# Operands moved within a 512-byte line: input tiles 256 bytes and activations 128 bytes off the weights, yt and yo level with them

## The chip, the cores and the metric

The kernel runs on one core of one Trainium2 chip. The metric is device time in microseconds (us). TensorE (PE in the profile) does the matmuls, VectorE (DVE), ScalarE (ACT) and GpSimd (POOL) the elementwise work, SyncE (SP) issues most DMAs. On-chip memory, SBUF, has 128 partitions, and a tile has the same byte address in each of them. This document speaks of the place of a tile as its address modulo 512, "its byte in a 512-byte line", and of the offset of a matmul as the place of its moving operand less the place of its weights, modulo 512.

## The reference

Two layers of a decoder trunk on x of 512 tokens by 1024 channels, all in float32:

```python
for l in range(DEPTH):                                   # DEPTH = 2
    x = x + 0.5 * swiglu(rms_norm(x, ffn1_norm[l]), ffn1_w_up[l], ffn1_w_down[l])
    h = rms_norm(x, mix_norm[l])
    q, k, v, z, xbc, dt_raw, gate_sb, gate_ssm = jnp.split(h @ w_in[l], IN_SPLITS, axis=-1)
    y_sb  = stick_breaking_attention(q, k, v) @ w_branch_sb[l]       # 4 heads of 128
    y_ssm = mamba2_mixer(z, xbc, dt_raw, ...) @ w_branch_ssm[l]      # 24 heads of 64, 8 groups
    x = x + (sigmoid(gate_sb) * y_sb + sigmoid(gate_ssm) * y_ssm) @ w_out[l]
    x = x + 0.5 * swiglu(rms_norm(x, ffn2_norm[l]), ffn2_w_up[l], ffn2_w_down[l])
return rms_norm(x, final_norm)
# swiglu: gate, up = split(h @ w_up); (silu(gate) * up) @ w_down, 2816 hidden channels
```

## The kernel before, in words

All activations lie with channels on the partitions and the 512 tokens in the free dimension, in blocks of 128 channels. A float32 matrix product is made of three matmuls in a reduced float32 format (`mm3`, lines 315 to 317): each operand is split into a high part and a low part, and high x high, low x high and high x low are accumulated. `mm(ps, a, b)` takes a as the weights, which are loaded into TensorE, and b as the moving operand, which streams through. While one matmul streams, the weights of the next are loaded.

The weights of the model come as a list of units (`unit_order`), a unit being up to 8 blocks of 128x128. Each is fetched to a tile wraw and split by ScalarE into whi (line 282) and by VectorE into wlo (line 284), a few units ahead of their use. `dense` runs a unit: for each block k, `mm3` with the unit's block k as weights and the moving pair of block k. The order of the work is written out by hand; generators that are stepped once a block (`tick`) put the elementwise work between the matmuls.

What moves against the weights, stage by stage:

- the first products of a feed-forward part, the q, k, conv and gate projections: the pair hhi, hlo of the normed input, 512 columns; the attention starts from them
- the rest of the up-projection (`pair_of_blocks`), which works on halves of 256 tokens with combined blocks: hhi and hlo, and the pair th, tl of combined inputs (`combine`), 256 columns
- the down-projection of a feed-forward part: the pair act, act, 512 columns (256 in the last three units, `ending`)
- the branch products: yt (the gated output of the state-space part, twelve pairs) and ohi, olo (of attention, pool yo), 512 columns; yt also holds q, k and v before
- the output projection: mhi, mlo, 512 columns
- v and z (`by_tokens`): here the input pair hhi, hlo is the weights and whi, wlo the moving operand, 512, 408 or 384 columns. For each block of 128 tokens, k = 0 and k = 1 follow each other, and the second lies `pitch` elements further in the unit; in the z block of 408 columns that is 448 elements, 1792 bytes.

Pools are stacked in SBUF from both sides, so the size of each tile sets the place of all that are stacked on it. In the built program they come to lie so (byte in a 512-byte line):

| tiles | before | after |
|---|---|---|
| whi, wlo, wraw | 96 | 96 |
| hhi, hlo, and acc, rs, sq, nones, ntri, upto | 96 | 352 |
| act, and s1, s2, s3, a, c, g of the feed-forward part | 96 | 224 |
| yt, ohi, olo | 480 | 96 |
| th, tl, uv, x | 480 | 480 |
| mhi, mlo, and bT, cT, btok, dec, xs, y of the mixer | 96 | 96 |

Of the kernel before, what the change touches and what calls it, by code (L numbers as in the profile page):

```python
# [8 lines left out]
F32 = mybir.dt.float32  # L9
# [8 lines left out]
P = 128  # L18
SEQ = 512
NT = SEQ // P  # L20
DM = 1024
# [142 lines left out]
class Builder:  # L164
# [298 lines left out]
    def consts(self):  # L463
        nc = self.nc
        c = self.cst
        self.ident = c.tile([P, P], F32, name="ident")
        make_identity(nc, self.ident)
        self.ones = c.tile([P, P], F32, name="ones")
        nc.vector.memset(self.ones, 1.0)
        self.eps = c.tile([P, 1], F32, name="eps")  # L470
        nc.vector.memset(self.eps, EPS)
        self.nones = c.tile([P, P], F32R, name="nones")
        self.ntri = c.tile([P, P], F32R, name="ntri")
        with self.tc.tile_pool(name="cst_tmp", bufs=1, reuse_waits="tile") as tp:
            neg = tp.tile([P, P], F32, name="neg")
            nc.vector.memset(neg, -1.0)
            nc.vector.tensor_copy(self.nones, neg)
            tri = tp.tile([P, P], F32, name="tri")
            nc.gpsimd.affine_select(out=tri, in_=neg, pattern=[[-1, P]], compare_op=ALU.is_ge, fill=0.0,
                                    base=0, channel_multiplier=1)  # L480
            nc.vector.tensor_copy(self.ntri, tri)
        self.upto = c.tile([P, P], F32, name="upto")
        nc.gpsimd.affine_select(out=self.upto, in_=self.ones, pattern=[[1, P]], compare_op=ALU.is_ge, fill=0.0,
                                base=0, channel_multiplier=-1)


    def rsqrt_small(self, v, y):
# [187 lines left out]
    def ending(self, base, act, n, fp):  # L675


        nc, half = self.nc, SEQ // 2
        blocks, units, squares, self.closing = OUT_ORDER[-3:], {}, {}, False
        gain = self.pars[0][:, G_FIN:G_FIN + KB]  # L680

        def block(m, ps, cols):
            x = self.x[m][:, cols]
            nc.vector.scalar_tensor_tensor(x, ps, 0.5, x, op0=ALU.mult, op1=ALU.add)
            yield 1
            sq = self.t(fp, [P, SEQ], "g", bufs=4)[:, :half]
            nc.scalar.activation(sq, x, AF.Square)
            self.closing = m == KB - 1 and cols.start
            if m == KB - 1:
                squares[cols.start] = sq  # L690
                return
            yield 1
            acc = self.acc[:, cols]
            nc.vector.tensor_tensor(acc, acc, sq, op=ALU.add)

        def finish(cols):
            ps = self.t(self.ptr, [P, SEQ], "pt")[:, :half]
            nc.tensor.matmul(ps, self.ones, self.acc[:, cols], start=True, stop=False)
            nc.tensor.matmul(ps, self.ones, squares[cols.start], start=False, stop=True)
            y = self.t(fp, [P, SEQ], "c", bufs=2)[:, :half]  # L700
            t, v = (self.t(fp, [P, SEQ], "a")[:, :half] for _ in range(2))
            nc.scalar.activation(y, ps, AF.Ln, scale=1.0 / DM, bias=self.eps)
            nc.scalar.activation(y, y, AF.Exp, scale=-0.5)
            nc.vector.tensor_scalar(v, ps, 1.0 / DM, EPS, op0=ALU.mult, op1=ALU.add)
            yield 2
            nc.vector.tensor_tensor(t, y, v, op=ALU.mult)
            nc.vector.scalar_tensor_tensor(t, t, -0.5, y, op0=ALU.mult, op1=ALU.mult)
            nc.vector.scalar_tensor_tensor(y, t, 1.5, y, op0=ALU.add, op1=ALU.mult)
            for m in range(KB):
                if m == 2 and not cols.start:  # L710
                    while not self.closing:
                        yield 1
                if m % 2 == 0:
                    yield 1
                r = self.xg[m][:, cols]
                if m in blocks:
                    nc.vector.scalar_tensor_tensor(r, self.x[m][:, cols], gain[:, m:m + 1], y,
                                                   op0=ALU.mult, op1=ALU.mult)
                else:
                    nc.vector.tensor_tensor(r, r, y, op=ALU.mult)  # L720
                (nc.scalar if m % 2 and cols.start else nc.sync).dma_start(self.out[m][:, cols], r)

        for m in blocks:
            self.xg[m] = self.t(self.hp, [P, SEQ], "hhi", F32R).bitcast(F32)
        for h in range(2):
            cols = slice(h * half, (h + 1) * half)
            for i, m in enumerate(blocks):
                pool, tag = (self.pa, "pa") if h and i else (self.pmm, "mm")
                ps = self.t(pool, [P, SEQ], tag)[:, :half]
                if h == 0:  # L730
                    units[m] = self.unit(*base, m)
                hi, lo = units[m]
                for k in range(n):
                    ks = slice(k * P, (k + 1) * P)
                    self.mm3(ps, (hi[:, ks], lo[:, ks]), [a[:, cols] for a in act[k]], k == 0, k == n - 1)
                    if k % 2:
                        self.tick()
                self.spawn(block(m, ps, cols))
            if h == 0:
                self.spawn(finish(cols), 2)  # L740
        while half not in squares:
            self.tick()
        self.spawn(finish(slice(half, SEQ)))
        self.flush()

    def ffn(self, layer, f, gain, gain_next):
        tc = self.tc
        with tc.tile_pool(name=f"act{layer}{f}", bufs=8, reuse_waits="tile") as ap, \
                tc.tile_pool(name=f"sx{layer}{f}", bufs=2, reuse_waits="tile") as self.sx, \
                tc.tile_pool(name=f"ffn{layer}{f}", bufs=3, reuse_waits="tile") as fp:  # L750
            self.gated = {}
            for s, (j0, j1) in enumerate(SLICES):
                act = []
                last = s == len(SLICES) - 1
# [43 lines left out]
    def dt_stage(self, layer):  # L798
# [5 lines left out]
        x = self.dtx.rearrange("p h c -> p (h c)")  # L804
        raw = yield from self.take("raw")
        u, w, adt, cum_t = raw[:, :n], raw[:, n:2 * n], raw[:, 2 * n:3 * n], raw[:n, SEQ - P:]
        self.tok = self.t(self.nrm, [P, 4, HEADS, NT], "sq")
        dt, cum, grown, left = (self.tok[:, i].rearrange("p h c -> p (h c)") for i in range(4))
        na = self.t(mp, [P, HEADS], "na", bufs=1)
        self.tables(True)  # L810
        nc.scalar.activation(u, x, AF.Abs)
# [14 lines left out]
        yield 3  # L826
        pt = self.t(self.ptr, [P, SEQ], "pt")
        nc.tensor.matmul(pt[:, :n], self.upto, adt, start=True, stop=True)
        nc.tensor.matmul(pt[:, n:2 * n], self.ones, adt, start=True, stop=True)
        yield 2  # L830
        nc.vector.tensor_copy(cum, pt[:, :n])
        nc.vector.tensor_tensor(left, pt[:, n:2 * n], cum, op=ALU.subtract)
        self.ecb = self.t(mp, [P, HEADS, NT], "ecb", bufs=1)
        nc.scalar.activation(grown, pt[:, :n], AF.Exp)
        nc.scalar.activation(self.ecb.rearrange("p h c -> p (h c)"), pt[:, n:2 * n], AF.Exp)
        yield 2
        nc.scalar.activation(left, left, AF.Exp)
        pt = self.t(self.ptr, [P, SEQ], "pt")
# [266 lines left out]
    def ssd_group(self, layer, g):  # L1105
# [15 lines left out]
        def heads(ap):  # L1121
            return ap.rearrange("p (h d) -> p h d", d=HD)
# [27 lines left out]
        def inner(c):  # L1150
            pc = self.t(self.ptr, [P, SEQ], "pt")
            pu = pc[:, P:P + GW]
            nc.tensor.matmul(pc[:, :P], bt[:, span(c)], ct[:, span(c)], start=True, stop=True)  # L1153
            if c < NT - 1:
                nc.tensor.matmul(pu, btok[:, c, :], xws[c].rearrange("p h d -> p (h d)"), start=True, stop=True)  # L1155
                new = states[c] = self.t(mp, [P, GW], "state")
                if c:
                    nc.vector.tensor_tensor(heads(new), heads(states[c - 1]), wide(self.ecb[:, h0:h0 + HPG, c]),
                                            op=ALU.mult)
            yield 1  # L1160
            nc.vector.tensor_tensor(decs[c], pc[:, :P].unsqueeze(1).to_broadcast([P, HPG, P]), decs[c], op=ALU.mult)
            if c == 0:
                nc.vector.tensor_copy(states[c], pu)
            elif c < NT - 1:
                nc.vector.tensor_tensor(states[c], pu, states[c], op=ALU.add)
# [107 lines left out]
    def mixer(self, layer):  # L1273
# [13 lines left out]
        with ExitStack() as mix:  # L1287
            enter = mix.enter_context
            branches = ExitStack()
            self.yo = branches.enter_context(  # L1290
                tc.tile_pool(name=f"yo{layer}", bufs=SBH, side="right", reuse_waits="tile"))
            self.yt = branches.enter_context(
# [98 lines left out]
    def build(self):  # L1391
# [7 lines left out]
        self.pmm = enter(tc.tile_pool(name="pmm", bufs=4, space=PSUM))  # L1399
        self.pa = enter(tc.tile_pool(name="pa", bufs=2, space=PSUM))  # L1400
        self.ptr = enter(tc.tile_pool(name="ptr", bufs=2, space=PSUM))
        self.open_x()
        self.open_t()
        self.tt = [self.t(self.tp, [P, SEQ], "tl", bufs=KB) for _ in range(KB)]
# [3 lines left out]
        self.consts()  # L1408
        warm = self.t(self.ptr, [P, SEQ], "pt")
        for _ in range(8):  # L1410
            nc.tensor.matmul(warm[:, :P], self.ones, self.ones, start=True, stop=True)
        self.norm_start()
        for m in range(KB):
            self.spawn(self.norm_square(m), 16 + m)
# [118 lines left out]
```

## Time and profile before

| what | value |
|---|---|
| median of 3 runs | 2587.33 us (2587.18 to 2587.63) |
| the profiled execution, first to last instruction | 2586.9 us |
| TensorE busy | 2565.8 us, 99% of the span |
| weight loads busy | 2289.6 us, 89% |
| VectorE busy | 1752.7 us, 68% |
| ScalarE busy | 1281.7 us, 50% |
| mean HBM traffic | 129 GB/s |

The profile gives one execution; its only time is the span, which lies 0.4 us under the median of the runs, and sums over its rows are made against it. A row of the groups reads: line, engine, operation, out<-in by the program's names, shapes, count | busy time in us, mean ns of one | idle time of the engine before. PE is the matmul, PEld the weight load. A matmul's duration contains its passage through the array and overlaps with the next, so durations don't add up to the time; two durations of the same shape can be compared. A row of the view by stretches reads: stretch, its length, then for each engine busy us and, in brackets, the instructions that it holds, granted clock, DMA share and GB/s. A row of the time line: start in us, duration, engine, line, operation. A row of a tile: line, engine, operation, count: shortest/median/longest in ns, first and last start, forms.

### The profile page before, as it was taken

Reading aid. Unit: us, or ns where it says so; the run is one execution under the profiler, and the core shown is the slowest. Engines: PE = TensorE matmul, PEld = TensorE weight load, DVE = VectorE, ACT = ScalarE, POOL = GpSimd, SP = SyncE. Lnnn points to the kernel's source line nnn. Section 1 sums busy time; section 2 is a strip of 40 time slices with the busy share of each in tenths; the row PEclk is TensorE's granted clock in tenths of the full one; section 3 lists DMA queues with packets and bytes.
Section 4 is the critical chain, followed back from the end, with each engine's and each line's share of the span. In section 5 each row is a group of like instructions: output and inputs, shape, how many; then the busy total and the mean of one; then the engine's idle time right before and its main releaser. Section 6 shows DMA issues by size and latency. Waiting matters only on the chain.

```text
span 2586.9 us, 38169 instructions
## 1 busy us (share of the span) xinstructions
PE 2565.8 (99%) x15028; PEld 2289.6 (89%) x15028; DVE 1752.7 (68%) x2426; ACT 1281.7 (50%) x2103; POOL 499.3 (19%) x614
## 2 busy tenths in 40 slices
PE   9999999999999999999999999999999999999998
PEld 8898988888888889899998989888888888899997
DVE  8576875676664478586885858756666644776766
ACT  6343556655554255343653535566555533543444
POOL 0121201143341002121121312012433310022120
PEclk9999999999999999999999999999999999999999
DMA  6454442233333455545364544423333334456452
GB/s 188 132 157 138 131 138 87 99 103 110 103 107 105 132 161 140 167 139 162 108 180 139 155 143 136 136 74 109 98 106 107 111 112 135 153 141 172 140 163 78
DMA packets 104659, 335.76 MB, mean 130 GB/s; under 512 B 11872, under 2 KB 15392, under 8 KB 104480
## 3 DMA queue, kind: packets, MB, share of 16 engines
q1 hardware_dynamic: 92672, 292.84, 33.9%
q0 software_dynamic: 10944, 39.85, 8.6%
q8 instruction: 118, 1.93, 0.3%
q10 hardware_dynamic: 864, 0.64, 0.1%
q14 instruction: 61, 0.50, 0.1%
HBM read 320.60 MB, written 12.68 MB: 129 GB/s over the span
## 4 chain that ended last, share of the span: by engine, by line
PE 93%; DVE 4%; ACT 2%; issue 1%; DMA 0%; POOL 0%; DVEq 0%; SPq 0%; ACTq 0%
PE mm L315 26%; PE mm L317 25%; PE mm L316 25%; PE pa L316 3%; PE pa L317 3%; PE pa L315 3%; PE pa L1170 2%; DVE wlo L284 1%; PE pa L1172 1%; PE pt L854 1%; PE pt L1155 1%; DVE cv L1028 1%; PE pt L1153 1%; ACT whi L282 1%; PE pa L453 1%
## 5 line engine op out<-in xcount | busy, mean ns | idle before, releaser
L282 ACT CAST whi<-wraw 128x1024 fp32r<-128x1024 f32 (+3 forms) x440 | 434.8, 989 | 593.0 <-PE mm L317 492.5
L284 DVE TENSOR_TENSOR wlo<-wraw,whi 128x1024 fp32r<-128x1024 f32 (+3 forms) x440 | 538.9, 1225 | 168.8 <-ACT whi L282 167.3
L315 PE MATMUL mm<-hhi,whi 128*128 128x512 f32 (+1 forms) x1584 | 564.5, 356 | 0.0
L317 PE MATMUL mm<-hlo,whi 128*128 128x512 f32 (+1 forms) x1584 | 553.4, 349 | 0.4 <-DVE hlo L507 0.4
L316 PE MATMUL mm<-hhi,wlo 128*128 128x512 f32 (+1 forms) x1584 | 552.3, 349 | 0.0
L317 PEld LDWEIGHTS mm<-hlo,whi 128*128 128x128 f32 x1584 | 299.7, 189 | 40.4 <-DVE hlo L507 0.8
L316 PEld LDWEIGHTS mm<-hhi,wlo 128*128 128x128 f32 x1584 | 300.1, 189 | 34.4
L315 PEld LDWEIGHTS mm<-hhi,whi 128*128 128x128 f32 x1584 | 300.0, 189 | 34.4 <-ACT hhi L505 0.4
L284 DVE TENSOR_TENSOR wlo<-s,whi 128x1024 fp32r<-128x1024 f32 x152 | 235.2, 1562 | 60.3 <-ACT whi L282 60.3
L315 PE MATMUL mm<-act,whi 128*128 128x512 f32 (+1 forms) x710 | 273.9, 386 | 0.0
L317 PE MATMUL mm<-act,whi 128*128 128x512 f32 (+1 forms) x710 | 273.9, 386 | 0.0
L316 PE MATMUL mm<-act,wlo 128*128 128x512 f32 (+1 forms) x710 | 273.9, 386 | 0.0
L315 PE MATMUL mm<-th,whi 128*128 128x256 f32 x912 | 257.1, 282 | 0.0
L317 PE MATMUL mm<-tl,whi 128*128 128x256 f32 x912 | 256.7, 281 | 0.0
L316 PE MATMUL mm<-th,wlo 128*128 128x256 f32 x912 | 256.5, 281 | 0.0
L626 POOL TENSOR_TENSOR g<-g,rs 128x512 f32<-128x512 f32 x76 | 132.7, 1747 | 554.9 <-DVE g L633 536.0
L282 ACT CAST whi<-s 128x1024 fp32r<-128x1024 f32 x152 | 159.3, 1048 | 102.4 <-PE mm L317 60.7
L652 DVE SCALAR_TENSOR_TENSOR x<-mm,x 128x512 f32<-128x512 f32 x93 | 64.1, 689 | 196.0 <-PE mm L317 196.0
L254 POOL DMA_DIRECT2D s<-in_wflat_dram x76 | 65.8, 865 | 625.0 <-DMA s<-in_wflat_dram 331.3
L315 PEld LDWEIGHTS mm<-th,whi 128*128 128x128 f32 x912 | 172.1, 189 | 0.0
L316 PEld LDWEIGHTS mm<-th,wlo 128*128 128x128 f32 x912 | 171.8, 188 | 0.0
L317 PEld LDWEIGHTS mm<-tl,whi 128*128 128x128 f32 x912 | 171.7, 188 | 0.0
(306 smaller groups left out, 5094.6 us busy)
## 6 DMA issues: line engine op xcount, KB each, us to landing
wraw<-in_wflat_dram SPq DMA_DIRECT2D x328, 512.0 KB, 3.6
s<-in_wflat_dram SPq DMA_DIRECT2D x76, 512.0 KB, 4.6
s<-in_wflat_dram POOLq DMA_DIRECT2D x76, 512.0 KB, 7.4
wraw<-in_wflat_dram SPq DMA_DIRECT2D x88, 384.0 KB, 3.1
cumb<-cum_d SPq DMA_DIRECT2D x16, 768.0 KB, 4.8
xd<-x SPq DMA_DIRECT2D x16, 256.0 KB, 3.3
wraw<-in_wflat_dram SPq DMA_DIRECT2D x16, 256.0 KB, 3.3
x<-xd SPq DMA_DIRECT2D x16, 256.0 KB, 3.8
```

What stands on the lines that cost most here:

```text
L254: self.nc.gpsimd.dma_start(raw, src, accum_op=ALU.add)
L282: nc.scalar.copy(hi[:, :n], raw[:, :n])
L284: nc.vector.tensor_tensor(lo[:, :n], raw[:, :n], hi[:, :n].bitcast(F32), op=ALU.subtract)
L315: mm(ps, a[0], b[0], start=start, stop=False, **kw)
L316: mm(ps, a[1], b[0], start=False, stop=False, **kw)
L317: mm(ps, a[0], b[1], start=False, stop=stop, **kw)
L453: nc.tensor.matmul(p, parts[a][:, ks], h[b], start=k + a + b == 0, stop=k == KB - 1 and b == 1)
L626: eng.tensor_tensor(r, r, self.rs[:, cols].unsqueeze(1).to_broadcast([P, 2, half]), op=ALU.mult)
L652: self.nc.vector.scalar_tensor_tensor(x, pd, 0.5, x, op0=ALU.mult, op1=ALU.add)
L854: self.nc.tensor.transpose(pt[:, cs], src[:, cs], self.ident)
L1028: nc.vector.scalar_tensor_tensor(u[:, j:], ps[:, :SEQ - j], tap[KCONV - 1 - j], u[:, j:], op0=ALU.mult, op1=ALU.add)
L1170: nc.tensor.matmul(py[:, i * HD:(i + 1) * HD], decs[c][:, i, :], xdts[c][:, i, :], start=True, stop=True)
```

## The change

It changes places only. Gap tiles, which nothing writes or reads, shift what is stacked on them: one of 256 bytes among the constants and one of 256 bytes ahead of wraw, so that the constants, the norm tiles and hhi, hlo come 256 bytes lower against the weights, which keep their address; one of 128 bytes ahead of act; one of 384 bytes at the right side under yo and yt. Room for it comes from the tile of ones, which is dropped (the minus ones take its place, with the sign taken back in a scale), and from the tile ecb, which becomes a fifth band of the tile of dt's other values. On every engine the instructions stand in the order of before, but for the memset of the ones, which now stands behind the other constants of VectorE, into a temporary tile. On SP, the first reload of a gate in the mixer waits for one more semaphore and the first two reloads of x for one less, because other tiles now lie over each other there.

```diff
@@ consts @@
-        self.ones = c.tile([P, P], F32, name="ones")
-        nc.vector.memset(self.ones, 1.0)
+        self.t(c, [P, 64], "gap")
...
-        self.upto = c.tile([P, P], F32, name="upto")
-        nc.gpsimd.affine_select(out=self.upto, in_=self.ones, ...)
+            one = tp.tile([P, P], F32, name="one")
+            nc.vector.memset(one, 1.0)
+            self.upto = c.tile([P, P], F32, name="upto")
+            nc.gpsimd.affine_select(out=self.upto, in_=one, ...)
+        self.minus = self.nones.bitcast(F32)
@@ ending: finish @@
-            nc.tensor.matmul(ps, self.ones, self.acc[:, cols], start=True, stop=False)
-            nc.tensor.matmul(ps, self.ones, squares[cols.start], start=False, stop=True)
+            nc.tensor.matmul(ps, self.minus, self.acc[:, cols], start=True, stop=False)
+            nc.tensor.matmul(ps, self.minus, squares[cols.start], start=False, stop=True)
...
-            nc.scalar.activation(y, ps, AF.Ln, scale=1.0 / DM, bias=self.eps)
+            nc.scalar.activation(y, ps, AF.Ln, scale=-1.0 / DM, bias=self.eps)
...
-            nc.vector.tensor_scalar(v, ps, 1.0 / DM, EPS, op0=ALU.mult, op1=ALU.add)
+            nc.vector.tensor_scalar(v, ps, -1.0 / DM, EPS, op0=ALU.mult, op1=ALU.add)
@@ ffn @@
             self.gated = {}
+            self.t(ap, [P, 32], "gap", bufs=1)
@@ dt_stage @@
-        self.tok = self.t(self.nrm, [P, 4, HEADS, NT], "sq")
-        dt, cum, grown, left = (...)
+        self.tok = self.t(self.nrm, [P, 5, HEADS, NT], "sq")
+        dt, cum, grown, left, ecb = (...)
...
-        nc.tensor.matmul(pt[:, n:2 * n], self.ones, adt, start=True, stop=True)
+        nc.tensor.matmul(pt[:, n:2 * n], self.minus, adt, start=True, stop=True)
...
-        nc.vector.tensor_tensor(left, pt[:, n:2 * n], cum, op=ALU.subtract)
-        self.ecb = self.t(mp, [P, HEADS, NT], "ecb", bufs=1)
+        nc.vector.scalar_tensor_tensor(left, pt[:, n:2 * n], -1.0, cum, op0=ALU.mult, op1=ALU.subtract)
...
-        nc.scalar.activation(self.ecb..., pt[:, n:2 * n], AF.Exp)
+        nc.scalar.activation(ecb, pt[:, n:2 * n], AF.Exp, scale=-1.0)
@@ ssd_group: inner @@
-                    nc.vector.tensor_tensor(heads(new), heads(states[c - 1]), wide(self.ecb[:, h0:h0 + HPG, c]),
+                    nc.vector.tensor_tensor(heads(new), heads(states[c - 1]), wide(col(4, c)),
@@ mixer @@
+            edge = branches.enter_context(
+                tc.tile_pool(name=f"edge{layer}", bufs=1, side="right", reuse_waits="tile"))
+            self.t(edge, [P, 96], "edge")
@@ build @@
+        self.t(self.wraw, [P, 64], "gap", bufs=1)
...
-            nc.tensor.matmul(warm[:, :P], self.ones, self.ones, start=True, stop=True)
+            nc.tensor.matmul(warm[:, :P], self.minus, self.minus, start=True, stop=True)
```

More of the change, by code (lines that the diff above doesn't have):

```diff
@@ L481, in consts @@
             nc.vector.tensor_copy(self.ntri, tri)
-        self.upto = c.tile([P, P], F32, name="upto")
-        nc.gpsimd.affine_select(out=self.upto, in_=self.ones, pattern=[[1, P]], compare_op=ALU.is_ge, fill=0.0,
-                                base=0, channel_multiplier=-1)
+            one = tp.tile([P, P], F32, name="one")
+            nc.vector.memset(one, 1.0)
+            self.upto = c.tile([P, P], F32, name="upto")
+            nc.gpsimd.affine_select(out=self.upto, in_=one, pattern=[[1, P]], compare_op=ALU.is_ge, fill=0.0,
+                                    base=0, channel_multiplier=-1)
+        self.minus = self.nones.bitcast(F32)
     def rsqrt_small(self, v, y):
@@ L806, in dt_stage @@
         u, w, adt, cum_t = raw[:, :n], raw[:, n:2 * n], raw[:, 2 * n:3 * n], raw[:n, SEQ - P:]
-        self.tok = self.t(self.nrm, [P, 4, HEADS, NT], "sq")
-        dt, cum, grown, left = (self.tok[:, i].rearrange("p h c -> p (h c)") for i in range(4))
+        self.tok = self.t(self.nrm, [P, 5, HEADS, NT], "sq")
+        dt, cum, grown, left, ecb = (self.tok[:, i].rearrange("p h c -> p (h c)") for i in range(5))
         na = self.t(mp, [P, HEADS], "na", bufs=1)
@@ L828, in dt_stage @@
         nc.tensor.matmul(pt[:, :n], self.upto, adt, start=True, stop=True)
-        nc.tensor.matmul(pt[:, n:2 * n], self.ones, adt, start=True, stop=True)
+        nc.tensor.matmul(pt[:, n:2 * n], self.minus, adt, start=True, stop=True)
         yield 2
         nc.vector.tensor_copy(cum, pt[:, :n])
-        nc.vector.tensor_tensor(left, pt[:, n:2 * n], cum, op=ALU.subtract)
-        self.ecb = self.t(mp, [P, HEADS, NT], "ecb", bufs=1)
+        nc.vector.scalar_tensor_tensor(left, pt[:, n:2 * n], -1.0, cum, op0=ALU.mult, op1=ALU.subtract)
         nc.scalar.activation(grown, pt[:, :n], AF.Exp)
-        nc.scalar.activation(self.ecb.rearrange("p h c -> p (h c)"), pt[:, n:2 * n], AF.Exp)
+        nc.scalar.activation(ecb, pt[:, n:2 * n], AF.Exp, scale=-1.0)
         yield 2
```

## The prediction

> **What bounds the kernel now.** I read the page first, then the waits of TensorE, then the groups with shapes kept apart, then stretches of time that hold matmuls of one kind only.
>
> ```profile
> span 2586.9 us, 38169 instructions
> PE 2565.8 (99%) x15028; PEld 2289.6 (89%) x15028; DVE 1752.7 (68%) x2426; ACT 1281.7 (50%) x2103; POOL 499.3 (19%) x614
> PEclk9999999999999999999999999999999999999999
> PE 93%; DVE 4%; ACT 2%; issue 1%; DMA 0%; POOL 0%; DVEq 0%; SPq 0%; ACTq 0%
> ```
>
> TensorE is busy 99% of the span at the full granted clock, and 93% of the chain that ended last is TensorE. In the list of TensorE's own waits there are eight rows, 10.1 us together; the first and the last are:
>
> ```profile
> PE pt L854 <- DVE cv L1040: 4.8, 8, 0.8
> ...
> PE pt L699 <- ACT g L687: 0.2, 1, 0.2
> ```
>
> So nothing that VectorE, ScalarE or a DMA could give back is worth more than about 10 us, and a nanosecond more on each matmul lands on the time almost whole. The change keeps every matmul and moves only the places of its operands. The question is therefore whether the distance from one start to the next (the pitch below) depends on where the moving tile lies against the weights. The groups show that it may:
>
> ```profile
> L316 PE MATMUL mm<-hhi,wlo 128*128 128x512 f32 x976 | 380.3, 390 | 0.0
> L316 PE MATMUL mm<-act,wlo 128*128 128x512 f32 x686 | 267.1, 389 | 0.0
> L316 PE MATMUL mm<-mhi,wlo 128*128 128x512 f32 x128 | 49.8, 389 | 0.0
> L316 PE MATMUL mm<-yt,wlo 128*128 128x512 f32 x192 | 75.8, 395 | 0.0
> L316 PE MATMUL mm<-ohi,wlo 128*128 128x512 f32 x64 | 25.3, 395 | 0.0
> L316 PE MATMUL pa<-hhi,wlo 128*128 128x512 f32 x32 | 12.4, 389 | 0.0
> L316 PE MATMUL mm<-hhi,wlo 128*128 128x256 f32 x608 | 172.0, 283 | 0.0
> L316 PE MATMUL pa<-hhi,wlo 128*128 128x256 f32 x304 | 85.8, 282 | 0.0
> L316 PE MATMUL mm<-th,wlo 128*128 128x256 f32 x912 | 256.5, 281 | 0.0
> ```
>
> Each row is one of three lines (315, 316, 317) with the same count. The weights whi and wlo lie at byte 96 of a 512-byte line. So do hhi, act and mhi (offset 0): 389 to 390 ns at 512 columns. Tiles yt, ohi and th lie at byte 480, an offset of 384: 395 ns at 512 columns, 6 more, but 281 against 283 at 256. These durations overlap; the pitch comes from stretches that hold one kind alone, length by number of matmuls in the code (the rows count a few more, which straddle the edges).
>
> ```profile
> 29.96:73.48 43.52, 43.52 (x193) 36.05 (x192) 37.12 (x57) 25.19 (x37) 1.89 (x2) 1.00 0.49 143
> 73.48:79.23 5.75, 5.75 (x49) 5.75 (x48) 3.63 (x4) 3.10 (x4) 0.00 (x0) 1.00 0.01 3
> 79.23:87.78 8.55, 8.55 (x74) 8.55 (x73) 6.74 (x6) 4.64 (x6) 3.50 (x2) 1.00 0.20 61
> 888.46:905.26 16.80, 16.80 (x74) 13.51 (x72) 7.92 (x10) 4.38 (x5) 0.00 (x0) 1.00 0.45 145
> 905.26:948.79 43.53, 43.53 (x193) 36.04 (x192) 32.35 (x48) 24.79 (x36) 0.00 (x0) 1.00 0.41 139
> 1031.06:1074.63 43.57, 43.57 (x194) 36.04 (x193) 18.85 (x21) 9.57 (x10) 1.74 (x2) 1.00 0.54 165
> ```
>
> In order: hhi 512 wide, 43.52/192 = 226.7 ns; hhi 256 wide, 5.75/48 = 119.8; th 256 wide, 8.55/72 = 118.8; yt, 16.80/72 = 233.3; mhi, 43.53/192 = 226.7; act, 43.57/192 = 226.9. The stretch of yt follows that of mhi on the same weights' buffers, and the other engines are busier in the second (VectorE 32.35 of 43.53 us, against 7.92 of 16.80), so traffic of other engines does not explain the 6.6 ns. I take the offset as the cause.
>
> The Trainium skill says otherwise: its page "SBUF — State Buffer", section "SBUF: two separate sides", has that "PE, ACT, and DVE's dedicated pair never wait on anyone". By that rule no place in SBUF costs TensorE anything, the sum below is 0 and the time stays; the 233.3 beside 226.7 speaks against it, and it stands as a rival below.
>
> **The change, part by part.**
>
> *yt and yo, offset 384 to 0.* yt moves 576 matmuls (192 on each of three lines), ohi and olo 192 (64 on each), all 512 wide. At offset 0 they should run at the 226.7 of mhi: 768 x (226.7 - 233.3) = -5.1 us. This is the one part whose two ends are both measured in this profile on the same shape.
>
> *act, offset 0 to 128.* 3 x 686 = 2058 matmuls of 512 columns. No long stretch has offset 128, but attention has short ones: there the moving tile (bT, at 96) meets v as weights (yt, at 480), and 96 - 480 is 128 within 512.
>
> ```profile
> 417.93 0.40 PE L315 MATMUL pt<-bT,yt 128*128 128x512 f32 x1
> ...
> 418.63 0.34 PE L315 MATMUL pt<-cT,yt 128*128 128x384 f32 x1
> L315 PE MATMUL pt<-bT,yt x8: 388/404/404, 417.9 to 1774.9; 128*128 128x512 f32 x8
> L316 PE MATMUL pt<-bT,yt x8: 392/395/395, 418.2 to 1775.1; 128*128 128x512 f32 x8
> L317 PE MATMUL pt<-bT,yt x8: 392/392/393, 418.4 to 1775.3; 128*128 128x512 f32 x8
> ```
>
> Three matmuls in 0.70 us are 233 ns each, and the medians of duration (404, 395, 392) are those of yt or above, never the 389 of act. These are runs of three only, so they may be the passage from one steady pitch to another; but they come out at what 384 gives, and 128 and 384 are the same distance from the weights' place, on its two sides. Bounds: 0 (the offset costs nothing in a long run) and +6.4 ns (yt's 233.3 less act's 226.9). I take the upper end, the one that the nearest rows show: 2058 x 6.4 = +13.2 us. Down units stand one behind the other with no wait on the list above, so nothing hides it.
>
> *hhi and hlo, offset 0 to 256.* 3 x 976 matmuls of 512 columns in mm and 3 x 32 in pa, 3024 in all; 3 x (608 + 304) = 2736 of 256. Offset 256 does occur before: in the first z block (408 columns, line 315 to 317 from `by_tokens`) the moving weights start at byte 96 for k = 0 and, 1792 bytes on, at 352 for k = 1, against hhi at 96. The triples alternate between 256 and 0:
>
> ```profile
> 432.06 0.35 PE L315 MATMUL mm<-whi,hhi 128*128 128x408 f32 x1
> ...
> 432.61 0.35 PE L315 MATMUL mm<-whi,hhi 128*128 128x408 f32 x1
> ...
> 433.16 0.35 PE L315 MATMUL mm<-whi,hhi 128*128 128x408 f32 x1
> ...
> 433.72 0.34 PE L315 MATMUL mm<-whi,hhi 128*128 128x408 f32 x1
> ```
>
> Triple at 256: 0.55 us; at 0: 0.55; at 256: 0.56. The two offsets cost the same to within 3 ns a matmul, the grain of these rows. I take 0 for hhi. The bounds are the shortest and the longest that the kinds show. Below:
>
> ```profile
> L315 PE MATMUL mm<-hhi,whi x64: 278/283/283, 1074.6 to 1140.1; 128*128 128x256 f32 x64
> L315 PE MATMUL mm<-act,whi x64: 387/389/397, 93.5 to 136.4; 128*128 128x512 f32 x64
> ```
>
> A 256-wide matmul was at best 5 ns shorter than its median (278 against 283), a 512-wide one 2 ns (387 against 389): 2736 x -5 = -13.7 us and 3024 x -2 = -6.0 us. Above: yt's pitch at 512 and th's at 256, 3024 x 6.6 = +20.0 and 2736 x -1.0 = -2.7, together +17.3 us. In `by_tokens`, where hhi becomes the weights at 352 and whi moves at 96, the offset is again 256, and the triples above stand for it.
>
> *The rest, with one answer: nothing.* th, tl and mhi keep their offsets. The 106 act matmuls of 256 columns in the ending, at th's gain, give -0.1 us; attention's v against its weights goes from 128 to 0 in 8 short groups, about 24 x -6 ns = -0.1 us. The ones become minus ones: the same count and shapes of matmuls, the sign taken back in an ACT scale or in a scalar_tensor_tensor that replaces a tensor_tensor. ecb moves into the tile of dt's other bands, written by the same ACT instruction. The warm-up now waits for nones (two memsets and a cast) in place of ones:
>
> ```profile
> 1.26 0.23 DVE L477 CAST nones<-neg 128x128 fp32r<-128x128 f32 x1
> ...
> 1.13 3.79 PE L1411 MATMUL pt<-ones 128*128 128x128 f32 x16 [1.13 <-DVE ones L469]
> 5.56 1.22 PE L453 MATMUL pa<-hhi,whi 128*128 128x512 f32 x2 [0.64 <-ACT hhi L505]
> ```
>
> It runs from 1.13 to 4.92 us; nones is there at 1.49, and sooner without the memset of ones. The first real matmul comes at 5.56 and waits for ScalarE, so 0.64 us cover a start that is at most 0.36 later. Without that cover it would cost those 0.36 us once. The queues of SP and POOL keep their order, and the chain gives DMA 0%. What follows a slower act is late by as much itself: the conversions of the next weights on ScalarE and VectorE gain slack, none is lost.
>
> **Sum.** -5.1 + 13.2 + 0 - 0.2 = +7.9 us on a span of 2586.9, so 2594.8. The median of the runs, 2587.33, lies 0.4 above the span: 2595.2 us, 0.3% slower.
>
> **The rivals.**
>
> *Only yt counts; act does not mind 128 in a long run.* For it: act's stretches also begin with longer matmuls (up to 397) and settle at 389, so attention's triples may be unsettled ones. Then 2587.3 - 5.1 = 2582.2. Chance 0.17.
>
> *Faster: an offset of half a line frees hhi.* If 256 holds every hhi matmul at the shortest seen, and 128 every act one, TensorE gains 13.7 + 6.0 + 2058 x 2 = 4.1 us, and 5.1 from yt: 2587.3 - 28.9 = 2558.4. With act as I forecast it is 2576. It beats no change as soon as hhi gains more than act loses less 5.1, 8.1 us, or 3 ns on each 256-wide matmul. Against it stand the equal triples. Chance 0.15.
>
> *Places cost TensorE nothing.* yt would be slow for a reason that stays when it moves (its tiles are scattered over 24 buffers, say). Then nothing changes: 2587.3. Against it: ohi and olo, eight tiles side by side at the same 480, have 395 too. Chance 0.07. This is what the rule that the Trainium skill's page "SBUF — State Buffer" gives would do here.
>
> *hhi suffers as yt did.* +17.3 on top: 2612.5. Chance 0.09.
>
> By the Trainium skill's page "TensorE: Matmul & The Clock Gate", section "Back-to-back issue gap", an isolated 512-wide matmul would follow the last after about 216 ns; by that figure a place without any cost would save 5082 x 10.9 = 55 us, an estimate that no row here reaches.
>
> **How the numbers follow.** The forecast has the rest, 0.52, with its own range of 2590 to 2597 (act between half and all of its 13.2 us). A measurement of this kernel tells about 0.2%, 5.2 us, from no change: 2582.2 to 2592.5 is the same. Faster: 0.15 of the second rival and half of the first, 0.09, are 0.24. Same: the other half, 0.08, the third, 0.07, and 0.03 of the forecast's lower end are 0.18. Slower: 0.49 and 0.09 are 0.58. The range from 2568 to 2604 leaves out about half of the faster rival and most of the last, some 0.15.
>
> **What would show it.** In the same stretches after: yt and ohi at 389 ns and 226.7 of pitch; act at 395 and 233; hhi unchanged at 389 to 390 and 283; th and mhi as before. The forecast is wrong if act stays at 389 or below (first rival), if hhi at 256 columns falls under 281 (second), if yt stays at 395 (third), or if hhi at 512 rises to 395 (last).

## The result, and the profile after

| | before | after |
|---|---|---|
| median of 15 runs each | 2587.18 us (2586.32 to 2588.61) | 2592.75 us (2592.26 to 2593.43) |
| ratio of the medians, 95% interval | | 1.002 [1.0014, 1.0027] |
| span of the profiled execution | 2586.9 us | 2590.6 us |

The change costs 5.57 us, 0.2%. The page of the kernel after differs from the page of before in little but TensorE's busy time (2565.8 us before):

```profile
span 2590.6 us, 38169 instructions
PE 2570.1 (99%) x15028; PEld 2290.8 (88%) x15028; DVE 1752.7 (68%) x2426; ACT 1281.5 (49%) x2103; POOL 499.4 (19%) x614
```

TensorE's groups, shapes kept apart (line, operation, out<-in, shape, count | busy us, mean ns of one | idle before):

```profile
L316 PE MATMUL mm<-hhi,wlo 128*128 128x512 f32 x976 | 380.7, 390 | 0.0
L316 PE MATMUL mm<-act,wlo 128*128 128x512 f32 x686 | 270.9, 395 | 0.0
L316 PE MATMUL mm<-th,wlo 128*128 128x256 f32 x912 | 256.9, 282 | 0.0
L316 PE MATMUL mm<-hhi,wlo 128*128 128x256 f32 x608 | 172.2, 283 | 0.0
L316 PE MATMUL mm<-yt,wlo 128*128 128x512 f32 x192 | 74.8, 389 | 0.0
L316 PE MATMUL mm<-ohi,wlo 128*128 128x512 f32 x64 | 24.9, 390 | 0.0
```

Act rose from 389 to 395 ns, yt and ohi fell from 395 to 389 and 390, hhi and th stayed. The same stretches as in the prediction (stretch, length, then busy us and instructions of each engine, granted clock, DMA share, GB/s), in order hhi of 512 columns (192 matmuls), hhi of 256 (48), th (72), yt (72), mhi (192), act (192):

```profile
28.20:71.72 43.52, 43.52 (x194) 36.06 (x193) 37.24 (x57) 25.39 (x37) 1.89 (x2) 1.00 0.53 145
71.72:77.47 5.75, 5.75 (x50) 5.75 (x48) 3.64 (x4) 3.10 (x4) 0.00 (x0) 1.00 0.01 3
77.47:86.02 8.55, 8.55 (x75) 8.55 (x74) 6.72 (x6) 4.63 (x6) 3.48 (x2) 1.00 0.20 61
887.57:903.89 16.32, 16.32 (x74) 13.53 (x72) 7.99 (x10) 4.41 (x5) 0.00 (x0) 1.00 0.43 145
903.89:947.41 43.52, 43.52 (x194) 36.06 (x192) 32.37 (x48) 24.78 (x36) 0.00 (x0) 1.00 0.41 139
1029.68:1074.29 44.61, 44.61 (x194) 36.22 (x193) 18.85 (x21) 9.56 (x10) 1.74 (x2) 1.00 0.55 164
```

Length by count: hhi 226.7 and 119.8 ns, th 118.8, mhi 226.7, all as before; yt 16.32 / 72 = 226.7 (233.3 before); act 44.61 / 192 = 232.3 (226.9 before).

Both traces hold all 15,028 matmuls in the same order, so the starts can be compared one by one. The 3.7 us between the two spans come out so:

| where | us |
|---|---|
| act, 512 columns, 0 to 128 | +11.1 |
| yt, ohi, olo, 384 to 0 | -4.9 |
| the first 19 us (clock and first data) | -1.8 |
| one wait at 1295 us, gone | -0.7 |
| all the rest together | -0.1 |

The wait is the passage from act to hhi at the start of a feed-forward part. Before, the list of TensorE's waits had this row, and two matmuls beside the wait were longer:

```profile
PE mm L317 <- DVE hlo L507: 0.4, 1, 0.4
```

After, the list has six rows and hlo is not among them: the slower act matmuls ahead of it give VectorE the time.

The start-up needs two stretches of time line (start us, duration, engine, line, operation). Before:

```profile
8.28 1.05 PE L453 MATMUL pa<-hhi,whi 128*128 128x512 f32 x2
9.14 0.99 PE L453 MATMUL pa<-hhi,wlo 128*128 128x512 f32 x2
9.97 0.62 PE L453 MATMUL pa<-hlo,whi 128*128 128x512 f32 x2
```

and after:

```profile
1.51 3.78 PE L1417 MATMUL pt<-nones 128*128 128x128 f32 x16 [1.51 <-DVE nones L476]
5.15 1.22 PE L453 MATMUL pa<-hhi,whi 128*128 128x512 f32 x2
6.17 0.73 PE L453 MATMUL pa<-hhi,wlo 128*128 128x512 f32 x2
6.74 0.62 PE L453 MATMUL pa<-hlo,whi 128*128 128x512 f32 x2
```

A pair of matmuls takes 1.05 us at first and 0.62 from some point on: in the trace of before, single matmuls start 427 ns apart at first and some 230 ns apart later. The record of TensorE's granted clock in the trace begins there, with 1.0 (full speed) from 9.92 us in the trace of before and from 6.38 in the other, where the row at 6.17 us holds one slow matmul and one fast one. The clock column of the view by stretches shows 1.00 before that too and can't be used for these microseconds. The profiled execution of before was not a usual one in this. In every run of these kernels the time is the span and about 1.7 us (2592.26 and 2590.6 in the profiled execution of after). So the profiled execution of before took 2588.6 us, and only 8 of 53 executions of before, over all the experiments, took more than 2588.2. Its span is 1.4 us above what the median implies, so the two spans understate the change, and the medians hold.

### The profile page after: what moved, and what is told of

Same layout as the page of the kernel before. It is cut to its first block, busy times and chain, and to the rows that moved or that the text cites. A ratio compares the mean times of both kernels' runs of the same rounds, so it can differ in the third digit from the quotient of the medians.

```text
span 2590.6 us, 38169 instructions
## 1 busy us (share of the span) xinstructions
PE 2570.1 (99%) x15028; PEld 2290.8 (88%) x15028; DVE 1752.7 (68%) x2426; ACT 1281.5 (49%) x2103; POOL 499.4 (19%) x614
## 4 chain that ended last, share of the span: by engine, by line
PE 93%; DVE 5%; ACT 2%; issue 1%; POOL 0%; DVEq 0%; ACTq 0%
PE mm L315 26%; PE mm L317 26%; PE mm L316 25%; PE pa L316 3%; PE pa L317 3%; PE pa L315 3%; PE pa L1172 2%; DVE wlo L284 1%; PE pa L1174 1%; PE pt L856 1%; PE pt L1157 1%; DVE cv L1030 1%; PE pt L1155 1%; ACT whi L282 1%; PE pa L453 0%
## 5 line engine op out<-in xcount | busy, mean ns | idle before, releaser
L315 PE MATMUL mm<-act,whi 128*128 128x512 f32 (+1 forms) x710 | 277.8, 391 | 0.0
L317 PE MATMUL mm<-act,whi 128*128 128x512 f32 (+1 forms) x710 | 277.7, 391 | 0.0
```

Source lines behind the costliest of these rows:

```text
L315: mm(ps, a[0], b[0], start=start, stop=False, **kw)
L317: mm(ps, a[0], b[1], start=False, stop=stop, **kw)
```

## The experiments

**Act put back.** The changed kernel without the gap ahead of act:

```diff
@@ ffn @@
-            self.t(ap, [P, 32], "gap", bufs=1)
```

> The changed kernel with act at byte 96 again, level with the weights (offset 0); all other places as in the changed kernel. Theory (the offset between moving operand and weights sets the pitch, and the pitches of the kinds add up): act falls from 232.4 to 226.9 ns, 2058 x 5.5 = 11.3 us, so 2592.75 - 11.3 = 2581.5 us, 0.22% under the kernel before. Rival (act's gap only moved a loss that the change would have had anyway, for instance because yt's gain is lost elsewhere in the median run): between 2585 and 2588 us, the time of before.

Measured: 2582.32 us against 2587.01 of before, ratio 0.998 [0.9972, 0.9989]; that is 10.4 under the changed kernel. The theory holds, a little under its 11.3 us, and the list of waits says why. Of its seven rows one is back:

```profile
PE mm L317 <- DVE hlo L509: 0.4, 1, 0.4
```

**Act alone.** The kernel before with that gap and nothing else:

```diff
@@ ffn @@
+            self.t(ap, [P, 32], "gap", bufs=1)
```

> The kernel before with one edit: act at byte 224, 128 off the weights. Theory: act at 232.4 ns, 2058 x 5.5 = +11.3 us, 2598.5 us, 0.44% slower. Rival (the rise of act in the changed kernel comes from the other moves): 2587 us.

Measured: 2597.52 us, ratio 1.004 [1.0027, 1.0052], +10.5. A stretch of 192 act matmuls:

```profile
1033.79:1078.40 44.61, 44.61 (x194) 36.17 (x193) 18.86 (x21) 9.55 (x10) 1.74 (x2) 1.00 0.54 162
```

Act has 232.3 ns of pitch here too, and hlo is again missing from the waits. The loss is act's own, less the wait that it hides.

**Yt alone.** The changed kernel with hhi and act both back at byte 96:

```diff
@@ consts @@
-        self.t(c, [P, 64], "gap")
+        self.t(c, [P, 128], "gap")
@@ ffn @@
-            self.t(ap, [P, 32], "gap", bufs=1)
@@ build @@
-        self.t(self.wraw, [P, 64], "gap", bufs=1)
```

> Only yt, ohi and olo at byte 96, level with the weights; hhi and act at 96 as before (the ones and ecb are dropped as in the change). Theory: 768 x -6.6 = -5.1 us, 2582.1 us; hhi at offset 256 costs nothing, so within 0.7 us of the kernel with act alone put back. Rival (offset 256 of hhi has a price or a gain that the sum of the changed kernel hides): the two differ by 1.5 us or more; at 0.5 ns on each of the 3024 matmuls of 512 columns it would be 1.5.

Measured: 2582.29 us, ratio 0.998 [0.9972, 0.9989], -4.7. Among the kinds that move against the weights it differs from the first experiment in hhi and hlo alone, offset 0 against 256, over 5760 matmuls, and by 0.03 us (the 11 runs of each kernel spread over 1.3 to 1.4 us). So the parts of the change are yt -4.7, act +10.5 and hhi 0.0, together 5.8 beside the 5.57 measured.

**The weights moved, not the moving tiles.** Up to here the weights always lay at byte 96, so the offset and the moving tile's own place could not be told apart. The kernel before with one gap:

```diff
@@ build @@
+        self.t(self.wraw, [P, 32], "gap", bufs=1)
```

> The kernel before with one gap of 128 bytes ahead of wraw: the weights lie at byte 224, and act, mhi and the mixer's tiles with them; hhi and hlo stay at 96, yt, ohi, th and tl at 480. Theory A (the offset to the weights counts): act and mhi stay at 226.7 to 226.9 ns (offset 0); hhi of 512 columns rises to 232 or 233 (offset 384), hhi of 256 falls from 120.0 to 118.7; yt and ohi fall to 226.7 and th rises to 120.0 (offset 256). In all 3024 x 6 - 2736 x 1.3 - 768 x 6.6 + 3648 x 1.3 = +14 us, 2601 us. Theory B (the place of the moving operand itself counts, 96 and 352 fast, 224 and 480 slow at 512 columns): act and mhi rise to 232.4, hhi, yt and th stay as they are: 2442 x 5.5 = +13.4 us, 2600.6 us. The pitch of each kind tells them apart, the time does not.

The time was 2597.26 us, 1.0037 [1.0023, 1.005]. The stretches, in the order used above (hhi 512, hhi 256, th, yt, mhi, act):

```profile
28.86:73.66 44.80, 44.80 (x194) 36.04 (x192) 37.32 (x57) 25.17 (x37) 1.88 (x2) 1.00 0.51 140
73.66:79.35 5.69, 5.69 (x50) 5.69 (x48) 3.60 (x4) 3.10 (x4) 0.00 (x0) 1.00 0.01 3
79.35:87.98 8.63, 8.63 (x74) 8.63 (x73) 6.80 (x6) 4.63 (x6) 3.49 (x2) 1.00 0.18 61
891.60:907.92 16.32, 16.32 (x73) 13.51 (x72) 8.00 (x10) 4.41 (x5) 0.00 (x0) 1.00 0.47 144
907.92:951.44 43.52, 43.52 (x193) 36.04 (x192) 32.37 (x49) 24.80 (x36) 0.00 (x0) 1.00 0.42 141
1034.40:1077.95 43.55, 43.55 (x195) 36.05 (x193) 18.83 (x21) 9.58 (x10) 1.74 (x2) 1.00 0.55 162
```

Hhi, which did not move, has 44.80 / 192 = 233.3 ns, and 118.5 at 256 columns; yt, which did not move, fell to 226.7; th, which did not move, rose to 119.9; mhi and act, which moved along with the weights, kept 226.7 and 226.8. This is theory A, kind by kind: the offset counts and the place does not. The total is 4 us under the 2601 expected. Most of that lies in the 2136 matmuls of hhi and hlo of 512 columns that stand in short runs between others: their mean pitch, without gaps over 300 ns, was 228.8 ns before and is 233.1 here, so they lose 4.3 ns and not 6.

**A map of offsets at 512 columns.** Act lies in a pool of its own in each of the four feed-forward parts, so one kernel tries four offsets:

```diff
@@ ffn @@
+            self.t(ap, [P, {(0, 1): 16, (0, 2): 48, (1, 1): 80, (1, 2): 112}[layer, f]], "gap", bufs=1)
```

> The kernel before with a gap of its own ahead of act in each of the four feed-forward parts: act lies 64, 192, 320 and 448 bytes off the weights, in that order of the parts. Theory (only the offset modulo 256 counts, and the price grows with the distance to the next multiple of 256): all four have the same distance, 64, and come out alike, about halfway at 229.5 ns for 512 columns. Rival 1 (any offset that is no multiple of 256 costs the same): 232 to 233 ns in all four. Rival 2 (the distance within 512 counts): 64 and 448 alike and low, 192 and 320 alike and high.

The second kernel has other sizes:

```diff
@@ ffn @@
+            self.t(ap, [P, {(0, 1): 64, (0, 2): 8, (1, 1): 56, (1, 2): 96}[layer, f]], "gap", bufs=1)
```

> The same with 256, 32, 224 and 384 bytes in the four parts. Theory (modulo 256, price by distance): 256 gives 226.7 ns, 32 and 224 alike at about 228, 384 as 128 or a little above, 232.4 to 233.3. Rival 1 (any but a multiple of 256 costs the same): 226.7, then three times 232 to 233. Rival 2 (distance within 512): 32 low, then 384, 224 and 256 rising, which the hhi of the changed kernel speaks against.

A stretch of 192 act matmuls in each part; first kernel (64, 192, 320, 448), then second (256, 32, 224, 384):

```profile
92.33:136.29 43.96, 43.96 (x194) 36.06 (x193) 18.86 (x21) 9.55 (x10) 1.73 (x2) 1.00 0.56 166
1031.19:1076.00 44.81, 44.81 (x195) 36.10 (x194) 18.85 (x21) 9.56 (x10) 1.74 (x2) 1.00 0.54 163
1377.94:1421.89 43.95, 43.95 (x194) 36.06 (x193) 18.85 (x21) 9.55 (x10) 1.74 (x2) 1.00 0.54 164
2316.82:2361.63 44.81, 44.81 (x195) 36.10 (x193) 18.86 (x21) 9.56 (x10) 1.74 (x2) 1.00 0.56 164
```

```profile
91.88:135.45 43.57, 43.57 (x195) 36.04 (x193) 18.85 (x21) 9.57 (x10) 1.73 (x2) 1.00 0.56 166
1029.44:1074.24 44.80, 44.80 (x195) 35.99 (x193) 18.85 (x21) 9.56 (x10) 1.74 (x2) 1.00 0.54 162
1376.23:1421.03 44.80, 44.80 (x194) 36.08 (x193) 18.85 (x21) 9.56 (x10) 1.74 (x2) 1.00 0.53 162
2317.20:2361.81 44.61, 44.61 (x194) 36.18 (x193) 18.85 (x21) 9.55 (x10) 1.74 (x2) 1.00 0.55 163
```

Divided by 192, the pitch is 229.0 ns at 64 and 228.9 at 320; 233.4 at 192 and at 448; 226.9 at 256; 233.3 at 32 and at 224; 232.3 at 384. The other long stretches of each part agree with the one shown to 0.1 ns. The two kernels took 2595.47 and 2595.50 us, in one run each, against 2587.53 of before. Half of my theory stood: only the offset modulo 256 counts (64 = 320, 192 = 448, 0 = 256). The other half fell: the price doesn't grow with the distance to a multiple of 256, since 32 costs 233.3 and 64 only 229, and 64 and 192 lie at the same distance and differ by 4.4. Both rivals fell too.

**The rest of the map, and the 256-column tiles.** First th and tl alone, moved by an edge pool of 96, 64 and 80 elements under the pool of th at its three openings:

```diff
@@ open_t @@
+        self.t_round = getattr(self, "t_round", -1) + 1
+        self.tedge = self.tc.tile_pool(name=self.name("tedge"), bufs=1, side="right", reuse_waits="tile")
+        self.t(self.tedge.__enter__(), [P, (96, 64, 80)[self.t_round]], "edge")
...
```

> The kernel before with th and tl (256 columns) moved: offset 0 in the first feed-forward part, 128 in the second and third, 64 in the fourth, in place of 384. Theory (at 256 columns the offset has the opposite sign, and again only the distance to a multiple of 256 counts): 120.0 ns at 0, 118.7 at 128 as at 384, between them at 64; about +2 us in all, 2589 us. Rival (384 alone is short): 120.0 in all three, +4.9 us, 2592 us.

Stretches of 72 th matmuls at 0, 128 and 64:

```profile
77.56:86.20 8.64, 8.64 (x75) 8.64 (x74) 6.78 (x6) 4.63 (x6) 3.51 (x2) 1.00 0.22 61
976.11:984.66 8.55, 8.55 (x74) 8.55 (x73) 6.75 (x6) 4.64 (x6) 5.10 (x4) 1.00 0.57 150
2257.80:2266.28 8.48, 8.48 (x74) 8.48 (x73) 6.72 (x6) 4.65 (x6) 5.12 (x4) 1.00 0.57 154
```

120.0, 118.8 and 117.8 ns. 0 and 128 as expected; 64 is not between them, it is the shortest. The time of the one run was 2587.27 us (2587.53 before, 2589 expected). Then act at 96, 160, 288 and 128 and th at 32, 96 and 160 in one kernel:

```diff
@@ ffn @@
+            self.t(ap, [P, {(0, 1): 24, (0, 2): 40, (1, 1): 72, (1, 2): 32}[layer, f]], "gap", bufs=1)
@@ open_t @@
...
+        self.t(self.tedge.__enter__(), [P, (88, 72, 56)[self.t_round]], "edge")
...
```

> Act lies 96, 160, 288 and 128 bytes off the weights in the four feed-forward parts, th and tl 32 in the first, 96 in the second and third, 160 in the fourth. From the offsets measured so far: act at 288 as at 32, 233.3 ns, and at 128 232.4 in the fourth part too; for 96 and 160 the rule that only a multiple of 256 and 64 past it are short gives 232 to 233.3. For th at 256 columns, 32, 96 and 160 between 117.8 and 120.0 ns. Rival (the pitch rises evenly from one multiple of 64 to another): act at 96 halfway between 228.9 and 232.4, 230.6. About 2587.2 + 2058 x 6.2 = 2600 us.

Act in that order, then th at 32, 96 and (two stretches) 160:

```profile
91.92:136.72 44.80, 44.80 (x195) 36.05 (x193) 18.87 (x21) 9.55 (x10) 1.74 (x2) 1.00 0.55 165
1032.74:1077.72 44.98, 44.98 (x194) 36.16 (x193) 18.82 (x21) 9.56 (x10) 1.74 (x2) 1.00 0.53 162
1381.14:1425.94 44.80, 44.80 (x195) 35.99 (x193) 18.82 (x21) 9.55 (x10) 1.74 (x2) 1.00 0.53 162
2322.49:2367.29 44.80, 44.80 (x195) 36.04 (x193) 18.87 (x21) 9.57 (x10) 1.74 (x2) 1.00 0.55 164
77.73:86.22 8.49, 8.49 (x75) 8.49 (x74) 6.71 (x6) 4.64 (x6) 3.49 (x2) 1.00 0.19 62
978.05:986.70 8.65, 8.65 (x75) 8.65 (x74) 6.79 (x6) 4.63 (x6) 5.12 (x4) 1.00 0.57 151
2268.37:2276.82 8.45, 8.45 (x74) 8.45 (x73) 6.71 (x6) 4.64 (x6) 5.12 (x4) 1.00 0.61 151
2288.26:2296.81 8.55, 8.55 (x75) 8.55 (x73) 6.92 (x6) 4.64 (x6) 5.18 (x4) 1.00 0.59 121
```

Act: 233.3, 234.3, 233.3, 233.3 ns. The rival's even rise (230.6 at 96) is out, and 160 lies above what I expected. At 128 the same offset gives 233.3 here and 232.3 in the changed kernel, which I had not expected. Th: 117.9 at 32, 120.1 at 96, and at 160 117.4 in one stretch and 118.8 in another. The time was 2600.82 us, as expected.

**Whose weights count.** While a matmul streams, the weights of the next are loaded. A gap between whi and wlo sets the two apart:

```diff
@@ opening @@
-            w.append((self.t(self.wsp, [P, KB * P], "whi", F32R), self.t(self.wsp, [P, KB * P], "wlo", F32R)))
+            hi = self.t(self.wsp, [P, KB * P], "whi", F32R)
+            if not w:
+                self.t(self.wsp, [P, 32], "gap", bufs=1)
+            w.append((hi, self.t(self.wsp, [P, KB * P], "wlo", F32R)))
```

> The kernel before with a gap of 128 bytes between whi (byte 96) and wlo (224); act, mhi and the mixer's tiles come to 224. Of the three matmuls of a block the first and the last use whi, the second wlo. Theory O (what counts is the offset to the weights that the matmul itself uses): hhi of 512 columns is slow in the second alone (232, others 226.7), act in the first and third. Theory L (what counts is the offset to the weights that are loaded while it streams, those of the next matmul): hhi is slow in the first alone (wlo is loaded then), act in the second and third (whi is loaded then). In both a third of hhi's and two thirds of act's matmuls are slow: about 2058 x 2/3 x 5.5 + 3024 / 3 x 4.5 = +12 us, 2599 us, so the pitches by position decide, not the time.

The matmuls of the first hhi stretch and of an act stretch, by tile (count: shortest/median/longest in ns, first and last start):

```profile
L315 PE MATMUL mm<-hhi,whi x65: 279/396/397, 30.7 to 75.1; 128*128 128x512 f32 x64, 128*128 128x256 f32 x1
L316 PE MATMUL mm<-hhi,wlo x64: 396/397/397, 31.0 to 74.6; 128*128 128x512 f32 x64
L317 PE MATMUL mm<-hlo,whi x64: 389/389/390, 31.2 to 74.9; 128*128 128x512 f32 x64
```

```profile
L315 PE MATMUL mm<-act,whi x64: 395/395/401, 1040.2 to 1084.3; 128*128 128x512 f32 x64
L316 PE MATMUL mm<-act,wlo x64: 396/397/398, 1040.5 to 1084.5; 128*128 128x512 f32 x64
L317 PE MATMUL mm<-act,whi x64: 390/393/394, 1040.7 to 1084.8; 128*128 128x512 f32 x64
```

This is neither theory: hhi is long on line 315 (its own weights level with it, those being loaded off) and on 316 (its own off, those being loaded level), and 389 only on 317, where both are level. From each start to the next, the three lines take 232.4, 234.3 and 226.6 ns. Act is off against at least one of the two on all three lines, and all three are long (232.5, 235.0 and 232.5 ns). A matmul keeps the short pitch only when both weights are level. So more are slow than either theory counted, and the time of the one run is 2609.62 us, +22 where I had +12; some 1.4 of the 22 are a late clock in this execution (10.61 us), an estimate from what it cost in two others. Why both weights count is open.

**Nine warm-up matmuls.** The kernel before with one more:

```diff
@@ build @@
-        for _ in range(8):
+        for _ in range(9):
```

> The kernel before with nine warm-up matmuls in place of eight, which ends the warm-up about 0.47 us later, at 5.4 us, closer to the first matmul that waits for data (5.1 to 5.6). Theory (an idle stretch of TensorE of some 0.6 us between the warm-up and the first matmul delays the full clock, from about 6.5 to about 9.9 us, as in the profiled execution of before): no execution with the late clock, all within 2586.3 to 2587.6, the median 0 to 0.5 us lower. Rival (the late clock comes at random): about a fifth of the executions at 2588.5 to 2589, as of before.

Measured: 2587.06 us, ratio 0.9999 [0.999, 1.0008]; the 11 executions lie between 2586.70 and 2587.82. In its trace the warm-up ends at 5.34 us, the first matmul follows at 5.41, and the full clock comes at 6.30. That none of the 11 took as long as an execution with the late clock speaks for the theory, but at 8 in 53 none would come up in 11 by luck one time in six; with the 37 executions of the three kernels whose warm-up starts later, where the longest is at most 0.9 us above its kernel's median, it is likelier. These runs do not settle it, and the median doesn't show it.

**The places that the map points to.** The kernel before with yt, ohi and olo at offset 256 and th, tl at 320; ones, ecb, hhi and act untouched:

```diff
@@ open_t @@
+        self.tedge = self.tc.tile_pool(name=self.name("tedge"), bufs=1, side="right", reuse_waits="tile")
+        self.t(self.tedge.__enter__(), [P, 16], "edge")
...
@@ mixer @@
+            edge = branches.enter_context(
+                tc.tile_pool(name=f"edge{layer}", bufs=1, side="right", reuse_waits="tile"))
+            self.t(edge, [P, 32], "edge")
```

> The kernel before with two gaps alone: 128 bytes under yo and yt (byte 352, offset 256 to the weights) and 64 bytes under th and tl (byte 416, offset 320); hhi and act stay level with the weights. Theory (the pitch depends on the kind's offset modulo 256 and on the width alone, and the pitches add up): yt, ohi and olo at 226.7 ns, -4.9 us as measured with yt alone moved; th and tl at the 117.8 that offset 64 gave, 3648 x -0.87 = -3.2 us; 2587.0 - 8.1 = 2578.9 us. Rival (th at 320 is not as at 64): 2582 us.

Measured: 2579.55 us against 2587.26, ratio 0.9971 [0.9959, 0.9982]: faster than both kernels, 7.7 us under before where 8.1 were expected. Its stretches of th (72) and yt (72):

```profile
77.59:86.07 8.48, 8.48 (x74) 8.48 (x73) 6.71 (x6) 4.65 (x6) 3.50 (x2) 1.00 0.20 62
884.33:900.65 16.32, 16.32 (x73) 13.52 (x72) 8.00 (x10) 4.41 (x5) 0.00 (x0) 1.00 0.49 147
```

117.8 and 226.7 ns: 320 is to th what 64 was, and yt is as well off at 256 as at 0.

## Why the prediction was right, and where its terms were off

The forecast of 2595.2 us was 2.45 above the 2592.75 measured, and its own range of 2590 to 2597 holds it; of the change itself it had +7.9 us where +5.57 came. The case that it named happened, in direction and place, by its own steps:

- *Places count.* The rival "places cost TensorE nothing" fell with yt and act. By the rule of the Trainium skill's page "SBUF — State Buffer", section "SBUF: two separate sides", that PE never waits on anyone, read as the prediction read it, both experiments with one part alone would have kept the time of before; they gave -4.7 and +10.5 us.
- *yt: -5.1 us.* Right: 226.7 ns as said, 4.9 us between the two traces, 4.7 in the runs with yt alone.
- *hhi: 0.* Right: 226.7 and 119.8 ns as before, 0.03 us between the two kernels that differ in it. The triples of 408 columns told it truly. The rivals "faster: half a line frees hhi" and "hhi suffers as yt did" fell; the bounds that they were priced by, -19.7 and +17.3 us, were far wider than needed.
- *act: +13.2 us.* The mechanism was right, the size too large: 232.3 and not 233.3 ns, 2058 x 5.4 = +11.1 us. I took yt's excess over act as the upper bound and the value. At this offset the long run settled on a pitch 1 ns shorter here, though on 233.3 in one part of another kernel. The short triples of attention had been read too high: their medians were called "those of yt or above", but the third, 392, is under yt's 395, and act now has a median of 393. The argument from the two sides ("128 and 384 are the same distance") came near the right number for a wrong reason, which is luck: distance does not set the price, the offset modulo 256 does, and 128 and 384 are the same in that. The rival "only yt counts" fell with act's 395 ns.
- *Nothing hides act.* Nearly: 0.7 us of it came back, because hlo's wait at 1295 us, on the list of waits at 0.4, vanished behind the slower act. I had read the list as an upper bound on gains and had not asked which of its rows a slower stage covers. With the measured parts in their places the sum is 7.9 - 2.1 (act) - 0.7 (the wait) + 0.2 (yt) + 0.1 (the rest, -0.1 and not -0.2) = 5.4 us.
- *The warm-up hidden.* Right: it starts 0.38 us later and costs nothing.
- *The base.* "The median of the runs lies 0.4 above the span" took the one profiled execution for a usual one. It was 1.4 us longer than usual, with its late clock, and every run adds about 1.7 to its span. In the sum this cancels, since the difference was laid on the median.

## What to carry to other kernels

Where TensorE is the bound and matmuls stand back to back, read the pitch (length of a stretch of one kind by its count) for each kind of moving tile and compare it with the byte offset between that tile and the weights, modulo 256: a pitch of 233.3 in place of 226.7 ns is 1.3 us on every 192 matmuls, and for yt a gap tile of 128 bytes was all that it took to get it back. Price a place by a long run at the same offset and the same width, for the order of the offsets differs between 512 and 256 columns. And before one profiled execution is made the base of a sum, see where its time lies among the others.

## What the runs showed of the hardware

The pitch of back-to-back float32 matmuls in the reduced format, in ns, by the offset of the moving tile to the weights modulo 256:

| columns | 0 | 32 | 64 | 96 | 128 | 160 | 192 | 224 |
|---|---|---|---|---|---|---|---|---|
| 512 | 226.7 to 226.9 | 233.3 | 228.9 to 229.0 | 233.3 | 232.3 or 233.3 | 234.3 | 233.4 | 233.3 |
| 256 | 119.8 to 120.0 | 117.9 | 117.8 | 120.1 | 118.5 to 118.8 | 117.4 or 118.8 | | |

At 512 columns the level place is the best, at 256 columns nearly the worst. All are from this one program on one core, most offsets from one kind of tile. The same offset can settle on two pitches, about 1 ns apart, and keep the one it fell into for a whole stretch; in the act stretch at offset 128 that has 233.3 ns, the starts are 229 and 238 ns apart by turns. What makes this was not found: the short pitch at 512 columns needs the weights in use and the weights being loaded to be level, and the experiments go no deeper.

By the traces' record of the granted clock, the full clock came at 4.0 to 6.7 us in ten of the thirteen executions whose profile I have, and at 9.7, 9.9 and 10.6 us in three. TensorE had stood idle for 0.59, 0.64 and 0.80 us between the warm-up and the first matmul in those three, and for at most 0.55 us in seven of the ten. In the other three it was 0.38, 0.67 and 0.78 us, but there the full clock had come before the idle time began (at 4.90, 4.04 and 4.49 us, with warm-ups that ended at 4.91, 4.55 and 4.76). So among the ten executions that were still at the lower clock then, 0.59 us or more went with a late clock every time, and 0.55 or less never did. One kernel alone was built to change that gap, so the cause is likely and not shown. A late clock goes with a longer time: the two such executions that can be set beside a median of their own kernel lie 1.3 and 1.4 us above it. The Trainium skill's page "TensorE: Matmul & The Clock Gate", section "What's actually happening", has a free-running activity window of about 3.4 us, and the full clock after a busy one. Taken back by that 3.4 us, the three late clocks come to 6.3, 6.5 and 7.2 us, an estimate, which agrees with windows that ended there, held the whole idle time and did not count as busy.
